# First feed-forward matrix in seven block products, its squares kept in DRAM, second matrix summed in eight PSUM banks

## The chip, the cores and the metric

The kernel runs on one core of a Trainium2 chip. The metric is the device time of one execution in microseconds (us). TensorE (PE in the profile) multiplies, VectorE (DVE), ScalarE (ACT) and GpSimd (POOL) work element by element, and SyncE (SP) issues nearly all transfers. PEld is TensorE's loading of the stationary operand, SPq the issuing of transfers on SP.

## The reference, cut to what matters

One layer of an encoder: three mixers, a gated merge, an output projection, then a feed-forward part and a final norm. Only the feed-forward part and its neighbours matter here:

```
x = x + merged @ w_out                       # (1024, 1024) @ (1024, 1024)
hf = rms_norm(x, ffn_norm_w)                 # 1024 tokens, 1024 features
x = x + square(relu(hf @ w_up)) @ w_down     # w_up (1024, 4096), w_down (4096, 1024)
return rms_norm(x, final_norm_w)
```

All of it is in float32.

## The kernel before

Every product of full precision is made of three passes. A float32 operand is split into a high part, which ScalarE casts (`L139`), and a low part, which VectorE or GpSimd gets by subtracting the high part from the original (`L140`). A matmul of operands a and b is then a-high b-high, a-high b-low and a-low b-high, summed in PSUM (`gemm_steps`, `gemm`). All matmuls go through `L81`, all transposes through `L84`, all transfers through `ld` on SP (`L97`).

The kernel is written as one list of operations. A planner simulates it and decides the order in which each engine runs its own; tiles are given out of pools with a fixed number of slots, and an operation that writes a tile waits until the slot's former tile has been read for the last time. Between `pe.pin = True` and `pe.pin = False` TensorE keeps the order of the program text.

**Output projection.** For each of eight blocks m of 128 tokens, 48 matmuls (two halves of 512 columns, eight k, three passes) give `x2`, to which the residual is added (`L1137`). `x2` is stored to `x2_d` in DRAM, squared and summed on ScalarE, and scaled in place by VectorE (`L1140`) into the normalised `hf`. `transposed(m, g)` then turns four 128 by 128 squares of it into one PSUM bank of the pool `ps_mm` (two banks) and splits them into `hfh` and `hfl`, in two pieces of 128 by 256: two casts on ScalarE, two subtractions on VectorE. I call one such call a turn. Eight turns (m = 0 to 3) are done inside the projection, the other eight between the first matmuls of the feed-forward part, one after every six matmuls.

**Feed-forward.** The 4096 hidden columns are cut into 32 tiles of 128, taken in 16 blocks of FB = 2. For each tile, `w_up`'s 1024 by 128 piece is loaded as `w_raw` (two slots) and split; `up` makes, for each half f of 512 tokens, 24 matmuls of 128 by 512 into one of six PSUM banks (`ps`), and then Relu on ScalarE (`L1159`), the square on VectorE (`L1160`) and the split into `ah`, `al`. The two matching 128 by 1024 rows of `w_down` are loaded as `w_raw` and split, the low part on GpSimd. `down` then makes, for each of eight token blocks and two column halves, six matmuls into a bank, and VectorE adds the bank to `o` in SBUF (`L1167`).

**End.** In the last block, after each `down`, ScalarE squares and sums `o` (`L1230`), GpSimd multiplies the first half by the final weight (`L1233`), `factor` makes the norm's factor, and `finish` scales the two halves (ScalarE, and VectorE in `L1183`) and stores them.

Pools: `U1` has 22 slots and `U2` 18 slots of 4 KB per partition; `wst` holds `w_raw`, `w_hi` and `w_lo`, two slots each; `sc` holds small working tiles (tags `g_l` and `g_t`, two slots each).

Of the kernel before, what the change touches and what calls it, by code (L numbers as in the profile page):

```python
# [24 lines left out]
FB = 2  # L25
# [45 lines left out]
class TensorE:  # L71


    def __init__(self, tc):
        self.tc, self.pin = tc, False
# [11 lines left out]
def hybrid_block(tc, x, mem, mix_norm_w, w_in, dn_conv_w, dn_a_log, dn_dt_bias, dn_norm_w, q_norm_w, k_norm_w,  # L87
# [107 lines left out]
    x2_d = [dram.tile([P, D], F32, name=f"x2_d{m}") for m in range(8)]  # L195

# [916 lines left out]
    hfh = [[None] * 4 for _ in range(2)]  # L1113
    hfl = [[None] * 4 for _ in range(2)]

    def transposed(m, g):
        t = slice((m % 4) * P, (m % 4 + 1) * P)
        ps = ps_mm()
        for j in range(4):
            pe.transpose(ps[:, j * P:(j + 1) * P], xs[m][:, (4 * g + j) * P:(4 * g + j + 1) * P], ident)  # L1120
        pv = ps.rearrange("p (k t) -> p k t", k=4)
        for q in range(2):
            split(hfh[m // 4][2 * g + q][:, :, t], hfl[m // 4][2 * g + q][:, :, t], pv[:, 2 * q:2 * q + 2])

    xs = []
    for m in range(8):
# [14 lines left out]
        if m % 4 == 3:  # L1141
            for k in range(4):
                hfh[f2][k] = ut("hfh", F32R, (P, 2, 512), True)
                hfl[f2][k] = ut("hfl", F32R, (P, 2, 512), True)
        if m >= 4:
            transposed(m - 4, 0)
            transposed(m - 4, 1)
# [3 lines left out]
    def up(w, f, ah, al_, between=()):  # L1151
        c = slice(f * 512, (f + 1) * 512)
        ps = ps2()
        pairs = [(w[0][:, k], w[1][:, k], hfh[f][k // 2][:, k % 2], hfl[f][k // 2][:, k % 2]) for k in range(8)]
        for i, _ in enumerate(gemm_steps(ps, pairs)):
            if i % 6 == 5 and between:
                transposed(*between.pop(0))
        r = sc.tile([P, 512], F32, name="f_r", tag="g_t")
        act.activation(out=r, in_=ps, func=AF.Relu)  # L1159
        dve.tensor_tensor(out=r, in0=r, in1=r, op=ALU.mult)  # L1160
        split(ah[:, c], al_[:, c], r)

    def down(m, c, a, wd):
        t = slice(m * P, (m + 1) * P)
        ps = ps2()[:, :c.stop - c.start]
        gemm(ps, [(a[k][0][:, t], a[k][1][:, t], wd[k][0][:, c], wd[k][1][:, c]) for k in range(FB)])
        dve.tensor_tensor(out=o[m][:, c], in0=o[m][:, c], in1=ps, op=ALU.add)  # L1167
# [22 lines left out]
    lwb = None  # L1190
    for blk in range(32 // FB):
        a, wu = [], []
        for ft in range(FB):
            wu.append(wunit(w_up[:, (blk * FB + ft) * P:(blk * FB + ft + 1) * P], 8, P))
            a.append((ut("ah", F32R), ut("al", F32R)))
            if blk > 0 or ft > 1:
                up(wu[ft], 0, *a[ft])
                up(wu[ft], 1, *a[ft])
            elif ft == 1:
                pe.pin = True  # L1200
                turns = [(m, g) for m in range(4, 8) for g in range(2)]
                up(wu[0], 0, *a[0], turns)
                up(wu[1], 0, *a[1], turns)
                pe.pin = False
                up(wu[0], 1, *a[0])
                up(wu[1], 1, *a[1])
        wd = []
        for k in range(FB):
            raw = wst.tile([P, 8, P], F32, name="w_raw", tag="w_raw").rearrange("p k c -> p (k c)")
            r = (blk * FB + k) * P  # L1210
            ld(out=raw, in_=w_down[r:r + P])
            two = blk % 2 == 1 and k == FB - 1
            wd.append((ut("wdh", F32R, two=two), ut("wdl", F32R, two=two)))
            split(*wd[k], raw, gp)
        if blk == 0:
            for m in range(8):
                o[m] = ut("o")
                ld(out=o[m], in_=x2_d[m])
        if blk == 32 // FB - 1:
            lwb = sc.tile([P, D], F32, name="lwb", tag="g_l")  # L1220
            ld(out=lwb, in_=final_norm_w.unsqueeze(0).broadcast_to([P, D]))
        for m in range(8):
            last = blk == 32 // FB - 1
            cs = (slice(0, 512), slice(512, 1024)) if not (last and m == 7) else (slice(0, 512), slice(512, 768), slice(768, 1024))
            if last:
                ss3[m] = sml.tile([P, 4], F32, name="ss3", tag="ss3", bufs=4)
            for j, c in enumerate(cs):
                down(m, c, a, wd)
                if last:
                    act.activation(out=sc.tile([P, 512], F32, name="jk3", tag="g_t")[:, :c.stop - c.start], in_=o[m][:, c],  # L1230
                                   func=AF.Square, accum_out=ss3[m][:, j:j + 1])
                    if j == 0:
                        gp.tensor_tensor(out=o[m][:, c], in0=o[m][:, c], in1=lwb[:, c], op=ALU.mult)  # L1233
            if last and m < 6:
                rs3[m] = factor(m, len(cs))
                finish(m)
    for m in (6, 7):
        rs3[m] = factor(m, len(cs) - 7 + m)
# [31 lines left out]
```

## Time and profile before

| | before |
|---|---|
| median of 3 runs | 1942.31 us (1937.68 to 1945.56) |
| profiled execution, its own time | 1945.84 us |
| its span, first to last instruction | 1944.0 us |
| mean granted TensorE clock | 0.989 |
| PE busy | 98% of the span, 10233 matmuls and transposes |
| DVE, ACT, POOL busy | 59%, 39%, 14% |
| DMA | 207.29 MB, mean 107 GB/s |

The span is the stretch that the profile covers; the profiled execution's time is 1.84 us longer. PE's busy time is the union of matmuls whose ends are modelled and which overlap, so the duration of one matmul is not what it costs; what it costs is the distance from one start to the next. The granted clock is given as a share of 2.4 GHz.

### The profile page before, as it was taken

How to read it: one execution, taken by the hardware profiler on the slowest of the kernel's cores; microseconds unless marked ns; L12 is line 12 of the kernel's file. 1: busy time of each engine (PE TensorE's matmuls, PEld its weight loads, DVE VectorE, ACT ScalarE, POOL GpSimd, SP SyncE). 2: the span in 40 equal slices, each digit the busy share in tenths (PEclk: the TensorE clock that was granted, in tenths of full speed). 3: DMA queues.
4: the chain of work that ended last, by engine and by line, in shares of the span. 5: the costliest groups of instructions: out<-in, count | busy, mean ns of one | idle time of the engine just before them, and what ended most of it. 6: DMA issues, size and time to landing. Idle time of an engine off the chain costs nothing.

```text
span 1944.0 us, 26261 instructions
## 1 busy us (share of the span) xinstructions
PE 1899.3 (98%) x10233; PEld 1609.5 (83%) x10233; DVE 1142.3 (59%) x1744; ACT 756.1 (39%) x1523; POOL 271.6 (14%) x230
## 2 busy tenths in 40 slices
PE   6999999999999999999999999999999999999997
PEld 5888778988988888888888878888888888888886
DVE  4677899993676666666635563444444434444446
ACT  4453434653546666666632131312121222112124
POOL 1003131231340000000001510101010101001013
PEclk8999999998999999999999999999999999999998
DMA  7235664566653222222255473311111202111113
GB/s 150 73 103 166 202 187 149 155 185 182 189 142 120 77 90 79 87 77 84 67 181 202 142 203 122 141 55 44 44 54 33 64 24 78 41 55 49 39 44 87
DMA packets 232750, 207.29 MB, mean 107 GB/s; under 512 B 44785, under 2 KB 196529, under 8 KB 232114
## 3 DMA queue, kind: packets, MB, share of 16 engines
q1 hardware_dynamic: 232306, 205.08, 35.1%
q8 instruction: 81, 1.33, 0.3%
q10 hardware_dynamic: 320, 0.52, 0.1%
q14 instruction: 43, 0.35, 0.1%
HBM read 148.39 MB, written 57.18 MB: 106 GB/s over the span
## 4 chain that ended last, share of the span: by engine, by line
PE 89%; DVE 4%; DMA 3%; issue 1%; ACT 1%; SPq 0%; POOL 0%; POOLq 0%; DVEq 0%; ACTq 0%
PE ps L81 40%; PE ps_mm L81 29%; PE ps_t L84 4%; PE ps_dn L81 4%; PE ps_sm L81 3%; PE ps_t L81 3%; PE ps_s L81 3%; PE ps_sp L81 2%; DMA xt<-in_x_dram 1%; DMA xs_d<-dd 1%; DMA w_raw<-in_w_out_dram 1%; DMA X<-xs_d 1%; DVE c_acc L409 1%; DVE o L1183 0%; SPq L97 0%
## 5 line engine op out<-in xcount | busy, mean ns | idle before, releaser
L81 PE MATMUL ps_mm<-hTh,w_hi 128*128 128x512 f32 x704 | 285.5, 406 | 5.2 <-ACT hTh L139 4.7
L81 PE MATMUL ps_mm<-hTl,w_hi 128*128 128x512 f32 x704 | 284.0, 403 | 0.0
L81 PE MATMUL ps_mm<-hTh,w_lo 128*128 128x512 f32 x704 | 277.5, 394 | 3.0 <-DVE w_lo L140 3.0
L1167 DVE TENSOR_TENSOR o<-o,ps 128x512 f32<-128x512 f32 (+1 forms) x257 | 170.9, 683 | 93.5 <-PE ps L81 92.7
L81 PE MATMUL ps<-hfh,w_hi 128*128 128x512 f32 x512 | 199.4, 391 | 0.0
L81 PE MATMUL ps<-wdh,al 128*128 128x512 f32 (+1 forms) x514 | 199.4, 388 | 0.0
L81 PE MATMUL ps<-wdl,ah 128*128 128x512 f32 (+1 forms) x514 | 199.4, 388 | 0.0
L81 PE MATMUL ps<-hfl,w_hi 128*128 128x512 f32 x512 | 199.3, 389 | 0.0
L81 PE MATMUL ps<-hfh,w_lo 128*128 128x512 f32 x512 | 199.3, 389 | 0.0
L81 PE MATMUL ps<-wdh,ah 128*128 128x512 f32 (+1 forms) x514 | 188.6, 388 | 0.0
L140 DVE TENSOR_TENSOR w_lo<-w_raw,w_hi 128x1024 fp32r<-128x1024 f32 x96 | 121.5, 1265 | 112.0 <-ACT w_hi L139 111.8
L1159 ACT ACTIVATE f_r<-ps 128x512 f32<-128x512 f32 x64 | 38.2, 597 | 358.9 <-PE ps L81 358.9
L139 ACT CAST w_hi<-w_raw 128x1024 fp32r<-128x1024 f32 x96 | 101.0, 1052 | 188.2 <-PE ps_mm L81 109.7
L1160 DVE TENSOR_TENSOR f_r<-f_r 128x512 f32<-128x512 f32 x64 | 55.4, 866 | 183.3 <-ACT f_r L1159 183.3
L140 POOL TENSOR_TENSOR wdl<-w_raw,wdh 128x1024 fp32r<-128x1024 f32 x32 | 76.3, 2395 | 601.4 <-ACT wdh L139 601.4
L81 PEld LDWEIGHTS ps_mm<-hTh,w_hi 128*128 128x128 f32 x704 | 133.5, 190 | 30.3 <-ACT hTh L139 5.1
L81 PEld LDWEIGHTS ps_mm<-hTh,w_lo 128*128 128x128 f32 x704 | 133.6, 190 | 28.7 <-DVE w_lo L140 3.2
L81 PEld LDWEIGHTS ps_mm<-hTl,w_hi 128*128 128x128 f32 x704 | 133.9, 190 | 20.8
L140 DVE TENSOR_TENSOR ptl<-ps_t,pth 128x512 fp32r<-128x512 f32 x128 | 86.6, 688 | 60.0 <-ACT pth L139 59.7
L81 PEld LDWEIGHTS ps<-wdh,ah 128*128 128x128 f32 x514 | 96.5, 188 | 20.5 <-DVE o L1167 0.6
L81 PEld LDWEIGHTS ps<-wdh,al 128*128 128x128 f32 x514 | 96.5, 188 | 19.8
L81 PEld LDWEIGHTS ps<-wdl,ah 128*128 128x128 f32 x514 | 96.4, 188 | 19.8
(288 smaller groups left out, 3838.3 us busy)
## 6 DMA issues: line engine op xcount, KB each, us to landing
w_raw<-in_w_in_dram SPq DMA_DIRECT2D x50, 512.0 KB
w_raw<-in_w_up_dram SPq DMA_DIRECT2D x32, 512.0 KB
w_raw<-in_w_down_dram SPq DMA_DIRECT2D x32, 512.0 KB
g_d<-gt SPq DMA_DIRECT2D x48, 256.0 KB
g_l<-g_d SPq DMA_DIRECT2D x24, 512.0 KB
w_raw<-in_w_branch_dram SPq DMA_DIRECT2D x12, 512.0 KB
y_raw<-y_d SPq DMA_DIRECT2D x12, 512.0 KB
xt<-in_x_dram SPq DMA_DIRECT2D x16, 256.0 KB
```

What stands on the lines that cost most here:

```text
L81: return self._put(self.tc.nc.tensor.matmul(*a, **k))
L84: return self._put(self.tc.nc.tensor.transpose(*a, **k))
L139: act.copy(out=hi, in_=src)
L140: (eng or dve).tensor_tensor(out=lo, in0=src, in1=hi.bitcast(F32), op=ALU.subtract)
L409: dve.scalar_tensor_tensor(out=acc[:, o], in0=xn[:, i], scalar=cw[:, ct, j:j + 1], in1=acc[:, o], op0=ALU.mult, op1=ALU.add)
L1159: act.activation(out=r, in_=ps, func=AF.Relu)
L1160: dve.tensor_tensor(out=r, in0=r, in1=r, op=ALU.mult)
L1167: dve.tensor_tensor(out=o[m][:, c], in0=o[m][:, c], in1=ps, op=ALU.add)
```

## The change

The first product, hidden = w_up transposed times hf transposed, is done by blocks. A unit u is a pair of tiles of hidden columns (256 columns, 16 units). Its weights are four blocks a11, a12 (first tile, feature halves) and a21, a22 (second tile), each 512 by 128; the tokens' side is four blocks b11, b21 (first 512 tokens, feature halves) and b12, b22 (second 512 tokens). Instead of eight block products there are seven, P1 to P7, of 12 matmuls of 128 by 512 each (four k, three passes). On the weights' side GpSimd makes four sums s1 to s4 per unit; on the tokens' side four sums T1 to T4 are made once, on GpSimd for the first two token blocks and on VectorE for the others. All seven weight blocks and seven token blocks are split into high and low parts: the token blocks stay in SBUF as `hs` (28 tiles, 16 in `U2` and 12 in `U1`), the weight blocks pass through the other slots of `U1`. Four token blocks now have two turns each as before (B11, B21), and 20 more turns (T3, T2, T1, B22, T4 for each of four blocks) stand between the 48 matmuls of P1 and P2 of the first two units, at a distance of four, three, two and two matmuls, in pinned order.

VectorE combines the products in `f_a` tiles: seven additions of a PSUM bank per unit, and four operations that do Relu and square at once. P1 is copied out by ScalarE. The two finished tiles of 128 by 1024 of a unit are stored to DRAM (`a_d`, 512 KB each). The first two units take P1 and P2 from a first load of one weight tile, and load both their tiles again for the rest.

The second product runs after the first is complete: for each half of 512 output columns, eight PSUM banks (six `ps2`, two `ps_mm`) hold the sums of the eight token blocks over all 32 k. Per k, the tile of `a_d` (512 KB) and the 128 by 512 piece of `w_down` (256 KB) are loaded and split, the latter's low part on GpSimd; k goes in groups of KG = 4, and within a group TensorE goes through the eight token blocks with 12 matmuls each. So `a_d` is read and split twice. `o` is added to once per block and half. In the last group of the second half, `factor` and `finish` follow each block; GpSimd's multiplication by the final weight is done in the first half only.

The diff, with the loops whose text is given above cut:

```diff
-    hfh = [[None] * 4 for _ in range(2)]
-    hfl = [[None] * 4 for _ in range(2)]
-    def transposed(m, g):
+    hs = {}
+    def turned(name, src, m):
+        if name not in hs:
+            hs[name] = [[ut("hs", F32R, (P, 2, 512), two=name in ("B11", "B21", "T3", "T2")) for i in range(2)] for _ in range(2)]
         ps = ps_mm()
         for j in range(4):
-            pe.transpose(ps[:, j * P:(j + 1) * P], xs[m][:, (4 * g + j) * P:(4 * g + j + 1) * P], ident)
+            pe.transpose(ps[:, j * P:(j + 1) * P], src[:, j * P:(j + 1) * P], ident)
...
+    turns = []
+    for m in range(4):
+        e = gp if m < 2 else dve
+        b11, b21, b12, b22 = xs[m][:, 0:512], xs[m][:, 512:1024], xs[m + 4][:, 0:512], xs[m + 4][:, 512:1024]
+        t3 = sc.tile([P, 512], F32, name="t3", tag="g_t")
+        e.tensor_tensor(out=t3, in0=b22, in1=b12, op=ALU.subtract)
+        e.tensor_tensor(out=b12, in0=b12, in1=b11, op=ALU.subtract)
+        e.tensor_tensor(out=b11, in0=t3, in1=b11, op=ALU.add)
+        e.tensor_tensor(out=b21, in0=b21, in1=b11, op=ALU.subtract)
+        turns += [("T3", t3, m), ("T2", b11, m), ("T1", b12, m), ("B22", b22, m), ("T4", b21, m)]
...
+    def halves(src, two=False):
+        w = ut("ws", F32R, (P, 2, 4, P), two=two)
+        split(w[:, 0], w[:, 1], src)
+        return w
...
+        gp.tensor_tensor(out=s1, in0=a21, in1=a22, op=ALU.add)
+        gp.tensor_tensor(out=s2, in0=s1, in1=a11, op=ALU.subtract)
+        gp.tensor_tensor(out=s3, in0=a11, in1=a21, op=ALU.subtract)
+        gp.tensor_tensor(out=s4, in0=a12, in1=s2, op=ALU.subtract)
+        for name, src in (("P6", s2), ("P2", a12), ("P7", s3), ("P4", a22), ("P5", s1), ("P3", s4)):
+            if name not in ws:
+                ws[name] = halves(src)
+    RHS = {"P1": "B11", "P2": "B21", "P3": "B22", "P4": "T4", "P5": "T1", "P6": "T2", "P7": "T3"}
+    def product(ws, name, between=(), every=4):
+        ps, w, (bh, bl) = ps2(), ws[name], hs[RHS[name]]
+        i = 0
+        for k in range(4):
+            for lw, rb in ((w[:, 0, k], bh), (w[:, 0, k], bl), (w[:, 1, k], bh)):
+                pe.matmul(ps, lhsT=lw, rhs=rb[k // 2][:, k % 2], start=i == 0, stop=i == 11)
+                i += 1
+                if i % every == 0 and between:
+                    turned(*between.pop(0))
+        return ps
+    def square(t):
+        dve.scalar_tensor_tensor(out=t, in0=t, scalar=0.0, in1=t, op0=ALU.max, op1=ALU.mult)
...
+        def rest(self):
+            r0, r1 = self.r0, ut("f_a", F32, (P, 2, 512), two=not self.lead)
+            add(r1[:, 1], r0[:, 1], product(self.ws, "P7"))
+            add(r1[:, 0], r1[:, 1], product(self.ws, "P4"))
+            square(r1[:, 0])
+            ps = product(self.ws, "P5")
+            add(r0[:, 1], r0[:, 1], ps)
+            add(r1[:, 1], r1[:, 1], ps)
+            square(r1[:, 1])
+            ld(out=a_d[2 * self.u + 1], in_=r1.rearrange("p f t -> p (f t)"))
+            add(r0[:, 1], r0[:, 1], product(self.ws, "P3"))
+            square(r0[:, 1])
+            ld(out=a_d[2 * self.u], in_=r0.rearrange("p f t -> p (f t)"))
+    pe.pin = True
+    lead = [Unit(0, True, "jk"), Unit(1, True)]
+    lead[0].p1(turns)
+    lead[1].p1(turns, 3)
+    lead[0].p2(turns, 2)
+    lead[1].p2(turns, 2)
...
+    for half in range(2):
+        c0 = half * 512
+        ps = [ps2() if m < 6 else ps_mm() for m in range(8)]
+        for kg in range(32 // KG):
+            a, wd = [], []
+            for k in range(kg * KG, (kg + 1) * KG):
+                raw = wst.tile([P, 8, P], F32, name="w_raw", tag="w_raw").rearrange("p k c -> p (k c)")
+                ld(out=raw, in_=a_d[k])
+                a.append((ut("ah", F32R, two=k % 2 == 0), ut("al", F32R, two=k % 2 == 0)))
+                split(*a[-1], raw)
+                raw = sc.tile([P, 512], F32, name="d_raw", tag="g_t")
+                ld(out=raw, in_=w_down[k * P:(k + 1) * P, c0:c0 + 512])
+                wd.append(ut("wd", F32R, (P, 2, 512), two=k % 2 == 1))
+                split(wd[-1][:, 0], wd[-1][:, 1], raw, gp)
...
-                down(m, c, a, wd)
+                        pe.matmul(ps[m][:, c], lhsT=ah[:, t], rhs=w[:, 0, c], start=kg == 0 and i == 0, stop=False)
+                        pe.matmul(ps[m][:, c], lhsT=ah[:, t], rhs=w[:, 1, c], start=False, stop=False)
+                        pe.matmul(ps[m][:, c], lhsT=al[:, t], rhs=w[:, 0, c], start=False, stop=last and i == KG - 1)
+                    dve.tensor_tensor(out=o[m][:, oc], in0=o[m][:, oc], in1=ps[m][:, c], op=ALU.add)
```

The eight loads of `o` from `x2_d` (512 KB each) move from the first feed-forward block to the start of the second product.

## Rows read from the trace of the kernel before

**Rows 1.** The page's busy times, and its chain of work that ended last
```profile
PE 1899.3 (98%) x10233; PEld 1609.5 (83%) x10233; DVE 1142.3 (59%) x1744; ACT 756.1 (39%) x1523; POOL 271.6 (14%) x230
...
PE 89%; DVE 4%; DMA 3%; issue 1%; ACT 1%; SPq 0%; POOL 0%; POOLq 0%; DVEq 0%; ACTq 0%
```
**Rows 2.** Stretches: busy us and count of PE, PEld, DVE, ACT, POOL; clock; DMA share, GB/s
```profile
1000.00:1100.00 100.00, 100.00 (x443) 82.79 (x442) 46.74 (x51) 18.79 (x19) 23.59 (x17) 1.00 0.52 173
1300.00:1400.00 100.00, 100.00 (x443) 82.81 (x442) 46.77 (x64) 19.43 (x27) 9.54 (x4) 1.00 0.18 53
...
1925.00:1944.00 19.00, 6.21 (x34) 5.19 (x32) 12.77 (x21) 8.86 (x23) 7.78 (x9) 0.74 0.63 166
```
**Rows 3.** TensorE in order of time, second product: a matmul and the twelfth after it
```profile
1400.05 0.39 PE L81 MATMUL ps<-wdh,al 128*128 128x512 f32 x1
...
1402.77 0.39 PE L81 MATMUL ps<-wdh,al 128*128 128x512 f32 x1
```
**Rows 4.** TensorE in order of time, two turns among first-product matmuls
```profile
1241.11 0.60 PE L84 MATMUL ps_mm<-ca,x 128*128 128x128 f32 x4
1241.46 0.48 PE L81 MATMUL ps<-hfh,w_hi 128*128 128x512 f32 x1
...
1242.93 0.60 PE L84 MATMUL ps_mm<-ca,x 128*128 128x128 f32 x4
1243.29 0.48 PE L81 MATMUL ps<-hfh,w_hi 128*128 128x512 f32 x1
```
**Rows 5.** ScalarE and VectorE in order of time, the split of one turn
```profile
1241.74 0.37 ACT L139 CAST hfh<-ps_mm 128x256 fp32r<-128x256 f32 x1 [0.33 <-PE ps_mm L84]
1242.61 0.38 ACT L139 CAST hfh<-ps_mm 128x256 fp32r<-128x256 f32 x1 [0.49 <-DVE hfl L140]
...
1243.02 0.42 DVE L140 TENSOR_TENSOR hfl<-ps_mm,hfh 128x256 fp32r<-128x256 f32 x1 [0.44 <-ACT hfh L139]
```
**Rows 6.** VectorE in order of time, three operations without a wait between
```profile
1132.14 0.69 DVE L140 TENSOR_TENSOR mgl<-g_acc,mgh 128x512 fp32r<-128x512 f32 x1
1132.74 0.69 DVE L1099 TENSOR_TENSOR g_acc<-g_acc,g_l 128x512 f32<-128x512 f32 x1
1133.34 0.68 DVE L1098 SCALAR_TENSOR_TENSOR g_l<-g_l,ps 128x512 f32<-128x512 f32 x1
```
**Rows 7.** GpSimd in order of time, one addition of 128 by 512 beside a busy VectorE
```profile
1108.67 1.62 POOL L1099 TENSOR_TENSOR g_acc<-g_acc,g_l 128x512 f32<-128x512 f32 x1 [1.81 <-DVE g_l L1098]
```
**Rows 8.** GpSimd and VectorE in order of time, about 1344
```profile
1341.03 4.75 POOL L140 TENSOR_TENSOR wdl<-w_raw,wdh 128x1024 fp32r<-128x1024 f32 x2 [41.17 <-ACT wdh L139]
...
1344.04 2.28 DVE L1160 TENSOR_TENSOR f_r<-f_r 128x512 f32<-128x512 f32 x1 [3.37 <-ACT f_r L1159]
```
**Rows 9.** A 512 KB load: its issue on SP, and the cast that waits for it
```profile
1118.69 0.33 SPq L97 DMA_DIRECT2D w_raw<-in_w_out_dram  x1
...
1123.11 1.05 ACT L139 CAST woh<-w_raw 128x1024 fp32r<-128x1024 f32 x1 [1.45 <-DMA w_raw<-in_w_out_dram]
```
**Rows 10.** Groups by shape between 1300 and 1900: busy us, mean ns
```profile
L140 DVE TENSOR_TENSOR w_lo<-w_raw,w_hi 128x1024 fp32r<-128x1024 f32 x27 | 33.1, 1225 | 57.4 <-ACT w_hi L139 57.4
...
L139 ACT CAST ah<-f_r 128x512 fp32r<-128x512 f32 x55 | 34.1, 621 | 62.0 <-DVE f_r L1160 62.0
```
**Rows 11.** VectorE in order of time: an addition, then what waits for its store
```profile
1228.85 0.69 DVE L1137 SCALAR_TENSOR_TENSOR x<-ps,x 128x512 f32<-128x512 f32 x1 [4.75 <-PE ps L81]
...
1232.92 1.29 DVE L1140 SCALAR_TENSOR_TENSOR x<-x,rs,fwb 128x1024 f32<-128x1024 f32 x1 [0.56 <-DMA x_d<-x]
```
**Rows 12.** The end in order of time: TensorE, ScalarE, VectorE
```profile
1930.93 0.28 PE L81 MATMUL ps<-wdh,al 128*128 128x256 f32 x1
...
1936.80 0.19 ACT L1230 ACTIVATION_READ_ACCUMULATOR jk<-o 128x1 f32 x1
...
1932.33 1.75 DVE L1183 SCALAR_TENSOR_TENSOR o<-o,rs,lwb 128x512 f32<-128x512 f32 x1
1934.01 0.68 DVE L1167 TENSOR_TENSOR o<-o,ps 128x512 f32<-128x512 f32 x1
...
1938.59 0.75 DVE L1183 SCALAR_TENSOR_TENSOR o<-o,rs,lwb 128x512 f32<-128x512 f32 x1 [0.73 <-POOL rs L136]
```

More of the change, by code (lines that the diff above doesn't have):

```diff
@@ L24 @@
 FILL = (3, 4, 5)
-FB = 2
+KG = 4
 LEAD = (12, 12)
@@ L195, in hybrid_block @@
     x2_d = [dram.tile([P, D], F32, name=f"x2_d{m}") for m in range(8)]
+    a_d = [dram.tile([P, S], F32, name=f"a_d{i}") for i in range(32)]
     ph1 = ExitStack()
@@ L1140, in hybrid_block @@
         dve.scalar_tensor_tensor(out=x2, in0=x2, scalar=rs, in1=fwb, op0=ALU.mult, op1=ALU.mult)
[L1141 to L1144, printed above, removed]
         if m >= 4:
-            transposed(m - 4, 0)
-            transposed(m - 4, 1)
-    o, ss3, rs3 = [None] * 8, {}, {}
[L1151 to L1167, printed above, removed]
+            turned("B11", xs[m - 4][:, 0:512], m - 4)
+            turned("B21", xs[m - 4][:, 512:1024], m - 4)
+    turns = []
[8 more added lines that the diff above has]
+        turns += [("T3", t3, m), ("T2", b11, m), ("T1", b12, m), ("B22", b22, m), ("T4", b21, m)]
@@ new lines, in add, with __init__, p1, p2 @@
+    def add(out, a, b):
+        dve.tensor_tensor(out=out, in0=a, in1=b, op=ALU.add)
+    def square(t):
+        dve.scalar_tensor_tensor(out=t, in0=t, scalar=0.0, in1=t, op0=ALU.max, op1=ALU.mult)
+    class Unit:
+        def __init__(self, u, lead=False, tag="g_l"):
+            self.u, self.ws, self.r0, self.lead = u, {}, None, lead
+            if lead:
+                raw = w_raw(2 * u)
+                self.ws = {"P1": halves(raw[:, 0:4], True), "P2": halves(raw[:, 4:8])}
+            else:
+                weights(u, self.ws)
+            self.t = sc.tile([P, 512], F32, name="f_t", tag=tag, **({"bufs": 1} if tag == "jk" else {}))
+        def p1(self, *a):
+            act.copy(out=self.t, in_=product(self.ws, "P1", *a))
+        def p2(self, *a):
+            ps = product(self.ws, "P2", *a)
+            self.r0 = self.r0 or ut("f_a", F32, (P, 2, 512), two=True)
+            add(self.r0[:, 0], self.t, ps)
+            square(self.r0[:, 0])
+        def p6(self):
+            ps = product(self.ws, "P6")
+            self.r0 = self.r0 or ut("f_a", F32, (P, 2, 512), two=True)
+            add(self.r0[:, 1], self.t, ps)
+        def rest(self):
[11 more added lines that the diff above has]
+            ld(out=a_d[2 * self.u], in_=r0.rearrange("p f t -> p (f t)"))
@@ L1169, in factor @@
+    pe.pin = True
[4 more added lines that the diff above has]
+    lead[1].p2(turns, 2)
+    for t in turns:
+        turned(*t)
+    pe.pin = False
+    for un in lead:
+        weights(un.u, un.ws)
+        un.p6()
+        un.rest()
+    for u in range(2, 16):
+        un = Unit(u)
+        un.p1()
+        un.p6()
+        un.p2()
+        un.rest()
     def factor(m, j):
@@ L1188, in finish @@
             ld_rows(o[m], out, m, store=True)
[L1190 to L1215, printed above, removed]
-            for m in range(8):
[L1217 to L1227, printed above, removed]
-                down(m, c, a, wd)
[L1229 to L1236, printed above, removed]
@@ L1237, in hybrid_block @@
     for m in (6, 7):
-        rs3[m] = factor(m, len(cs) - 7 + m)
+        rs3[m] = factor(m, 2)
     finish(7)
```

37 lines of the change are left out of this document (35 added, 2 removed).

## The prediction

> **What bounds the kernel now.** I read the busy times and the chain first, then stretches, then single instructions. The page puts 98% of the span and 89% of the chain on PE [rows 1]. In the feed-forward part, every stretch of 100 us that I asked for is full of PE work at a granted clock of 1.00, which is the 2.4 GHz level, with VectorE busy about 47 of 100 and the transfers at 18% [rows 2]. So TensorE sets the pace there, and a change is worth what it takes off or adds to TensorE, unless something else becomes late. The reader must not take a matmul's 0.39 us for its cost: starts lie 2.72 us apart over twelve matmuls, 0.2267 us each [rows 3], and 443 in 100 us say the same [rows 2]. Only at the very end is TensorE not the bound: its last matmul starts at 1930.93, and 13 us pass until the span's end, in which VectorE works off a backlog [rows 2, 12].
>
> **The first product.** Before: 32 tiles by two halves by 24 matmuls, 1536. After: 16 units by seven products by 12, 1344. That is 192 fewer, and 192 by 0.2267 is 43.5 us off. The second product keeps 1536 matmuls, all of 512 columns but for the last twelve, which were of 256; there only the order changes.
>
> The Trainium skill, page "TensorE: Matmul & The Clock Gate", section "Back-to-back issue gap", gives about 131 ns as the sustained distance for 512 columns. The trace shows 226.7 ns; by the page's figure the 192 matmuls would be worth 25 us and the forecast below 18 us higher, and I keep the measured one.
>
> **The turns.** There were 16, there are 28: the eight inside the projection stay, eight behind it become twenty. Two turns with six matmuls between start 1.82 us apart [rows 4]; six matmuls are 1.36, so a turn costs TensorE 0.46 us. Twelve more: plus 5.5 us.
>
> They also come closer together. On TensorE alone a turn would come every four, three or two matmuls: 1.37, 1.14 or 0.91 us. A turn's split alternates between ScalarE and VectorE: cast, subtraction, cast, subtraction, where the second cast waits for the first subtraction; from the transposes' start at 1241.11 to the last subtraction's end at 1243.44 it is 2.33 us [rows 4, 5]. With two banks that is one turn per 1.17 us if two turns overlap perfectly. For the sixteen turns of the three denser products the lag is then 4 by 0.03 plus 12 by 0.26, some 3 us. VectorE has other work in the same stretch: the last normalisation (1.3), four differences for the last token block (2.4), two additions and two squares (2.4), at 0.60 each [rows 6]; I let half of these 6 us fall into the chain: 6 us of stall in all. Its ends: none, if VectorE's other work falls between; and 15, if two turns don't overlap at all (20 by 1.73, the four conversions, against 20 us of TensorE work, that is 48 by 0.2267 plus 20 by 0.46).
>
> The token sums are otherwise covered: for the first two blocks GpSimd makes them while the projection still runs, where a block takes 48 by 0.2267, or 10.9 us, against four operations of up to 1.62 [rows 7]; the third block's fall in the same cover on VectorE.
>
> **The units.** A unit takes TensorE 84 by 0.2267, 19.0 us, and that must cover everything else. VectorE: seven low parts, seven additions, four squares, 18 at 0.60, 10.8 us [rows 6]. ScalarE: seven casts and a copy of 0.62 [rows 10], 5 us. GpSimd: four sums of up to 1.62, 6.5 us [rows 7]. Weights: `U1` keeps 10 slots beside the 12 token tiles, so a weight block can be written once the product ten before it is done and is wanted nine products, 24.5 us, later. Two loads one behind the other (4.4 us for a lone one [rows 9], some 7 for both), three sums (4.9) and a split (1.2) are 13 us. Results: `U2` keeps two slots. The earlier tile of a unit is stored after three VectorE operations behind P5 (1.8 us); a store of 512 KB lands at most 3.4 us after its data is ready [rows 11]; the next unit first writes its tile after P3, P1 and P6, 8.2 us. On SP the store waits for the square with the next loads of weights behind it, but those are wanted 24 us later. And should VectorE come late, six banks hold 16 us of products. So the units cost nothing beyond their matmuls. Without that cover, each us by which VectorE's unit passes 19.0 costs 16 us.
>
> **Between the products.** In the last unit, `o` takes eight slots of `U1` first; the second and fourth tile of `a_d` and the first and third of `w_down` get theirs only as P4 and P5 end. After P4, TensorE has P5 and P3 left, 5.4 us, then 2 us of matmuls per block on the first three k. In that time the second tile is split (2.3), the fourth loaded (4.4) and split (2.3): 9.0 against 7.4, and 4 MB of `o` run beside it. I take 5 us of stall; the ends are none (if tiles come free earlier) and 14 (four k served at 3.5 us each, the second product's service time below, with nothing ahead).
>
> **The second product.** A k takes TensorE 24 by 0.2267, 5.4 us, in each half. It needs 768 KB, 145 GB/s; between 1000 and 1100 the queues moved 173 GB/s at a share of 0.52 without holding up TensorE [rows 2]. A slot of `w_raw` is held for a load (4.4 [rows 9]), a cast and a subtraction (1.05 and 1.23 [rows 9, 10]) and an issue (0.33), 7.0 us; with two slots 3.5 us per k, under 5.4. ScalarE has 1.7 us per k, VectorE 1.2, GpSimd 1.6. Cost: nothing. VectorE loses 257 additions into `o` and gets 16; they lay beside TensorE, so that is worth nothing, except at the end.
>
> **The end.** Before, each block of the last group cost VectorE two additions, and a scaling that took 1.75 beside GpSimd's multiplication, 0.75 without it [rows 12]. After, in the second half, it is one addition, two tiny operations and 0.75, some 1.7 us, under TensorE's 2.72 per block. So the end follows the last matmul: its own 0.39, the addition 0.69, the square and sum 0.8, semaphores 0.1, and then from the end of the last sum at 1936.99 to 1944.0 as before, 7.0: 9.0 us instead of 13.1. Minus 4 us; ends minus 5 and nothing.
>
> **Sum.** −43.5 + 5.5 + 6 + 5 − 4 = −31.0. The profiled execution took 1945.84 and would take 1914.8; the median of the runs shown lies 3.5 below that execution, so I forecast 1911. With all ends favourable it is −43.0, 1899; with all unfavourable −9.5, 1933.
>
> **Rivals.** (1) VectorE becomes the bound of the units. For it: a VectorE operation with two SBUF inputs that started beside GpSimd's two took 2.28 us instead of 0.69 and ended with them [rows 8], so it waited for GpSimd. If all of GpSimd's 6.5 us per unit were lost to VectorE, 10.8 becomes 17.3, still under 19.0; waiting for weight sums in its queue would have to add the rest. At 21 us per unit it costs 31 us: 1942, no change.
> The Trainium skill, page "SBUF — State Buffer", section "Who interferes with whom", has this as a rule: the pair of ports is an exclusive lock, and the later instruction blocks fully. The trace agrees; by the rule alone the unit stays TensorE's.
> (2) The second product becomes bound by its loads, the other side. What it has against it is the count above; for it, that `a_d` is read back twice, loads and 4 KB rows share one queue with `w_down`'s, and the two slots leave no more than one load in flight while the other is split. It decides at a load of 8.2 us, 1.9 times the measured one; the forecast's gain is gone at 9.2. At 10 us a k takes 6.3 instead of 5.4, 64 times: plus 55, 1966.
> (3) The two seams are worse than my ends, because TensorE, starved for several us, also gets the clock that the last stretch shows after its last matmul (0.74 on average [rows 2]): 1938, no change.
> (4) A matmul costs its 0.39 us, and 192 are worth 75 us: 1880. The starts speak against it.
>
> **Chances.** Forecast 0.78 (own range 1899 to 1933); (1) 0.06; (2) 0.09; (3) 0.05; (4) 0.02. A difference under 0.5%, 9.7 us, can't be told from none. Faster 0.80, same 0.11, slower 0.09. From 1898 to 1936 leaves out (1), (2), (4) and half of (3), under 2 in 10.
>
> **What would show it.** In the profile after: 1344 first-product matmuls 0.227 apart, PE without idle time from the second unit to the last; in the stretch after the projection, idle TensorE before transposes, some 6 us; a gap of some 5 us where the second product begins; VectorE at 60 to 90% in the units and under 40% in the second product, where DMA stands near 150 GB/s; and some 9 us from the last matmul's start to the end. Casts of `a_d` tiles waiting for transfers with TensorE waiting behind them would show (2); TensorE waiting for VectorE's additions or low parts inside units, (1). The prediction is wrong if the planner's order puts a late operation ahead of an urgent one on a strictly ordered engine, which I can't see from the trace of before.

## The result, and the profile after

The changed kernel takes 1920.88 us (median of 4 runs, 1916.88 to 1923.65), beside 1943.47 us before on the same chip: a ratio of 0.9887, 95% interval 0.9857 to 0.9917. It is faster, by 22.6 us where 31 were forecast. The profiled executions say the same: spans of 1921.9 and 1944.0 us, 22.1 apart.

The page's busy times and chain after, to be held against [rows 1]:

```profile
PE 1869.7 (97%) x10083; PEld 1582.3 (82%) x10083; DVE 1154.8 (60%) x1727; ACT 801.6 (42%) x1609; POOL 405.0 (21%) x334
...
PE 88%; DVE 5%; DMA 3%; ACT 1%; issue 1%; POOL 0%; SPq 0%; POOLq 0%; DVEq 0%; ACTq 0%
```

Three stretches after, with the columns of [rows 2]: the turns behind the projection, the units up to the last one, the second product:

```profile
1229.20:1276.00 46.80, 34.56 (x152) 25.62 (x152) 32.49 (x62) 19.44 (x52) 13.20 (x9) 0.82 0.23 68
1276.00:1564.00 288.00, 287.88 (x1270) 238.39 (x1271) 205.07 (x278) 73.52 (x123) 84.11 (x58) 1.00 0.39 127
1564.00:1913.00 349.00, 348.96 (x1540) 288.40 (x1538) 99.20 (x100) 114.19 (x160) 114.85 (x77) 1.00 0.46 149
```

The second and third are full of TensorE work at the full clock. The first is not: TensorE is without work for 12.2 of 46.8 us, and its granted clock is 0.82 on average. Nearly all that the change gave back is there. TensorE in that stretch, in order of time (start, us, operation, and in brackets the idle time before it and what ended it):

```profile
1229.22 1.42 PE L81 MATMUL ps<-hs,ws 128*128 128x512 f32 x4
...
1232.87 0.60 PE L84 MATMUL ps_mm<-ca,x 128*128 128x128 f32 x4
1233.23 1.17 PE L81 MATMUL ps<-hs,ws 128*128 128x512 f32 x4
1238.14 1.08 PE L84 MATMUL ps_mm<-ca,x 128*128 128x128 f32 x4 [3.74 <-issue]
1238.87 1.63 PE L81 MATMUL ps<-hs,ws 128*128 128x512 f32 x3
...
1249.81 0.63 PE L84 MATMUL ps_mm<-ca,x 128*128 128x128 f32 x4 [1.94 <-issue]
```

Each gap stands before the four transposes of a turn: they wait for a bank whose last turn has not been split. (For the gap of 3.74 us the profile names no releaser; the low part that frees the bank ended at 1238.03, 0.11 us before the transposes.) After the gap of 3.74 us the same four transposes take 1.08 instead of 0.60 us and three matmuls 1.63 us, where three took 0.94 at the full clock (a row of a later run below): TensorE had gone to its 1.2 GHz level. VectorE and GpSimd at the longest gap, each in order of time:

```profile
1230.32 0.15 DVE L135 TENSOR_SCALAR rsq_t<-ss 128x1 f32<-128x1 f32 x1 [0.69 <-ACT jk L222]
...
1232.15 1.13 DVE L1153 TENSOR_TENSOR t<-x 128x512 f32<-128x512 f32 x1 [0.28 <-PE ps_mm L84]
1233.20 0.41 DVE L140 TENSOR_TENSOR hs<-ps_mm,hs 128x256 fp32r<-128x256 f32 x1
1233.54 1.44 DVE L1154 TENSOR_TENSOR x<-x,x 128x512 f32<-128x512 f32 x1
1235.42 2.28 DVE L1142 SCALAR_TENSOR_TENSOR x<-x,rs,fwb 128x1024 f32<-128x1024 f32 x1 [0.44 <-POOL rs L136]
1237.62 0.41 DVE L140 TENSOR_TENSOR hs<-ps_mm,hs 128x256 fp32r<-128x256 f32 x1
1237.96 1.42 DVE L1155 TENSOR_TENSOR x<-t,x 128x512 f32<-128x512 f32 x1
...
1245.61 0.69 DVE L1153 TENSOR_TENSOR t<-x 128x512 f32<-128x512 f32 x1 [0.41 <-PE ps_mm L84]
...
1231.44 1.29 POOL L1179 TENSOR_TENSOR w_s<-w_raw 128x512 f32<-128x512 f32 x1 [12.12 <-DMA w_raw<-in_w_up_dram]
1232.69 1.75 POOL L1181 TENSOR_TENSOR w_s<-w_raw 128x512 f32<-128x512 f32 x1
1234.39 0.99 POOL L136 TENSOR_TENSOR rs<-rsq_t,mhalf 128x1 f32<-128x1 f32 x1
1235.36 1.26 POOL L1180 TENSOR_TENSOR w_s<-w_s,w_raw 128x512 f32<-128x512 f32 x1
```

The low part that would free the bank is the one at 1237.62. Ahead of it on VectorE stand a difference of the third token block (`L1154`), stretched to 1.44 us, and the last normalisation (`L1142`), which waits for its factor and then takes 2.28 us. The factor (`L136` on GpSimd) had its input at 1230.47 and ran only at 1234.39, behind two weight sums, the first of which waited for its load until 1231.44. GpSimd runs its operations in the order that the planner gave it. The third block's first difference (`L1153`) ran only at 1232.15, released by transposes (`L84`): the tile t3 that it writes has two slots, and both held T3 of the first two blocks until the first was turned. The fourth block's waited in the same way until 1245.61.

The end after, in order of time, against [rows 12]:

```profile
1913.00 0.39 PE L81 MATMUL ps_mm<-wd,al 128*128 128x512 f32 x1
...
1913.99 0.68 DVE L1320 TENSOR_TENSOR o<-o,ps_mm 128x512 f32<-128x512 f32 x1
...
1915.23 0.19 ACT L1321 ACTIVATION_READ_ACCUMULATOR jk<-o 128x1 f32 x1
...
1916.53 0.75 DVE L1281 SCALAR_TENSOR_TENSOR o<-o,rs,lwb 128x512 f32<-128x512 f32 x1 [0.73 <-POOL rs L136]
```

From the last matmul's start to the span's end it is 8.9 us, where it was 13.1. VectorE keeps up: the scaling takes 0.75 us and follows its factor.

### The profile page after: what moved, and what is told of

The parts are those of the page before. It is cut to its first block, busy times and chain, and to the rows that moved or that the text cites. A ratio compares the mean times of both kernels' runs of the same rounds, so it can differ in the third digit from the quotient of the medians.

```text
span 1921.9 us, 26681 instructions
## 1 busy us (share of the span) xinstructions
PE 1869.7 (97%) x10083; PEld 1582.3 (82%) x10083; DVE 1154.8 (60%) x1727; ACT 801.6 (42%) x1609; POOL 405.0 (21%) x334
## 3 DMA queue, kind: packets, MB, share of 16 engines
q1 hardware_dynamic: 252818, 256.47, 43.5%
## 4 chain that ended last, share of the span: by engine, by line
PE 88%; DVE 5%; DMA 3%; ACT 1%; issue 1%; POOL 0%; SPq 0%; POOLq 0%; DVEq 0%; ACTq 0%
PE ps L81 34%; PE ps_mm L81 34%; PE ps_t L84 4%; PE ps_dn L81 4%; PE ps_sm L81 3%; PE ps_t L81 3%; PE ps_s L81 3%; PE ps_sp L81 2%; DMA xt<-in_x_dram 1%; DMA w_raw<-in_w_out_dram 1%; PE ps_mm L84 1%; DVE c_acc L410 1%; DMA xs_d<-dd 1%; DVE w_lo L140 0%; SPq L97 0%
## 5 line engine op out<-in xcount | busy, mean ns | idle before, releaser
L81 PE MATMUL ps<-hs,ws 128*128 128x512 f32 x1344 | 314.5, 394 | 0.3 <-ACT hs L139 0.2
L81 PEld LDWEIGHTS ps<-hs,ws 128*128 128x128 f32 x1344 | 253.0, 190 | 52.0 <-ACT hs L139 0.8
L81 PE MATMUL ps<-wd,ah 128*128 128x512 f32 x768 | 236.4, 389 | 0.0
L140 DVE TENSOR_TENSOR al<-w_raw,ah 128x1024 fp32r<-128x1024 f32 x64 | 83.7, 1309 | 208.5 <-ACT ah L139 116.0
L81 PEld LDWEIGHTS ps<-wd,ah 128*128 128x128 f32 x768 | 144.0, 188 | 30.5 <-POOL wd L140 0.8
L140 POOL TENSOR_TENSOR wd<-d_raw,wd 128x512 fp32r<-128x512 f32 x64 | 102.5, 1604 | 228.6 <-ACT wd L139 228.6
L81 PE MATMUL ps<-wd,al 128*128 128x512 f32 x384 | 148.9, 389 | 0.0
L139 ACT CAST pth<-ps_t 128x512 fp32r<-128x512 f32 x128 | 74.1, 584 | 49.1 <-PE ps_t L84 48.9
L900 ACT ACTIVATE pm<-ps_s,nmx 128x1024 f32<-128x1024 f32 x64 | 71.6, 1119 | 41.1 <-DVE nmx L899 41.1
L899 DVE TENSOR_REDUCE nmx<-ps_s 128x1 f32<-128x1024 f32 x64 | 78.2, 1221 | 17.5 <-PE ps_s L81 16.5
```

Of the source, the lines that this page charges most:

```text
L81: return self._put(self.tc.nc.tensor.matmul(*a, **k))
L139: act.copy(out=hi, in_=src)
L140: (eng or dve).tensor_tensor(out=lo, in0=src, in1=hi.bitcast(F32), op=ALU.subtract)
L899: dve.tensor_reduce(out=nmx, in_=ps, axis=AX.X, op=ALU.max, negate=True)
L900: act.activation(out=p_out, in_=ps, func=AF.Exp, bias=nmx, accum_out=sm)
```

## The experiments

The measure that they share is the loss: the time from the first matmul of the first product to the first of the second, less 1344 by 0.2267 and 20 by 0.46, that is less 313.9 us. In the changed kernel it is 1564.57 − 1229.22 − 313.9 = 21.5 us. Where the stretch begins differs by up to 9 us between the profiled executions (1220.6 to 1230.0); I compare stretches and not spans for that reason, and have not looked into what shifts it. "Waits" is TensorE's idle time with a releaser in the stretch, read from its timeline, and "longest" the longest of them. "Factor" is how long after the stretch's first matmul GpSimd began the last normalisation's factor. Times are medians, each ratio is to the kernel before on the same chip. Each loss is read from one profiled execution. Executions of one kernel lie up to 10 us apart (no differences: 1907.25 to 1917.25, the profiled one the slowest), and no run shows how much of that falls into the stretch, so small differences between losses prove nothing.

| run | us | ratio, interval | stretch from, to | loss | waits | longest | factor |
|---|---|---|---|---|---|---|---|
| changed kernel | 1920.88 | 0.9887, 0.9857 to 0.9917 | 1229.22, 1564.57 | 21.5 | 12.3 | 3.74 | 5.2 |
| t3 slots | 1913.30 | 0.9849, 0.9826 to 0.9872 | 1229.07, 1556.57 | 13.6 | 8.8 | 1.92 | 1.3 |
| no sums for the first units | 1913.28 | 0.9851, 0.9832 to 0.9870 | 1222.58, 1551.34 | 14.9 | 8.9 | 1.93 | 1.3 |
| four banks | 1910.64 | 0.9837, 0.9818 to 0.9857 | 1229.59, 1553.10 | 9.6 | 5.8 | 3.34 | 5.5 |
| no differences | 1911.58 | 0.9834, 0.9808 to 0.9860 | 1229.94, 1558.70 | 14.9 | 9.5 | 3.20 | 5.0 |
| no sums, no differences | 1906.26 | 0.9822, 0.9807 to 0.9838 | 1220.59, 1544.13 | 9.6 | 6.4 | 1.00 | 1.4 |
| slots and banks | 1904.28 | 0.9814, 0.9800 to 0.9829 | 1224.75, 1544.11 | 5.5 | 4.3 | 1.72 | 1.3 |
| and differences on GpSimd | 1907.04 | 0.9826, 0.9810 to 0.9843 | 1229.96, 1553.09 | 9.2 | 6.6 | 2.74 | 5.9 |
| slots, banks, spread | 1907.54 | 0.9825, 0.9800 to 0.9850 | 1227.78, 1547.82 | 6.1 | 4.9 | 1.73 | 1.3 |
| spread alone | 1913.68 | 0.9857, 0.9837 to 0.9877 | 1221.81, 1552.49 | 16.8 | 11.6 | 3.69 | 5.1 |

One thing differs between these runs that no edit was made for. In five of them, the changed kernel among them, the planner put the factor behind one or two weight sums, so that it came 5.0 to 5.9 us into the stretch, and there the longest wait is 2.74 to 3.74 us. In the other five it came after 1.3 or 1.4 us, and the longest wait is 1.00 to 1.93 us. No run moves the factor alone, so what its place is worth by itself is not shown; where an edit changed it, I say so.

**Slots for t3.**

```diff
-        t3 = sc.tile([P, 512], F32, name="t3", tag="g_t")
+        if m < 2:
+            t3 = sc.tile([P, 512], F32, name="t3", tag="g_t")
+        else:
+            t3 = wst.tile([P, 2, 4, P], F32, name="t3", tag=("w_hi", "w_lo")[m - 2])[:, 0].rearrange("p k c -> p (k c)")
```

> The changed kernel with one thing moved: the difference tile t3 of the third and fourth token block gets slots of its own (in the weight pool), so that its operations need not wait until the first two blocks' T3 have been turned. In the changed kernel the stretch from the first first-product matmul to the first second-product matmul is 336 us, of which 1344 matmuls at 0.2267 and 20 turns at 0.46 explain 314; 22 us are lost, all of them ahead of 1276 us. Theory A (the differences come late, in front of the low parts on VectorE, because t3 has two slots): the third block's four operations go back into the projection, the gaps of 3.7 and 1.9 us before transposes shrink, and 8 us or more of the 22 come back: about 1912 us. Theory B (GpSimd's weight sums lock VectorE out): 0 to 3 us. Theory C (two banks with an alternating split set the turns' rate whatever VectorE does): 0 to 3 us.

The loss fell by 7.9 us, nearly the 8 that theory A gave. That the differences come late because of t3's slots is shown: the third block's first one ran at 1221.16, inside the projection, and not 2.9 us into the stretch. That all of the 7.9 us comes from this is not shown, for with the slots the planner also put the factor ahead of the weight sums:

```profile
1230.40 0.55 POOL L136 TENSOR_TENSOR rs<-rsq_t,mhalf 128x1 f32<-128x1 f32 x1 [11.23 <-DVE rsq_t L135]
```

And 13.6 us stay.

**No weight sums for the first two units.**

```diff
+        if u < 2:
+            for name, src in (("P6", a21), ("P7", a11), ("P4", a22), ("P5", a21), ("P3", a22)):
+                ws[name] = halves(src)
+            return ws
         gp.tensor_tensor(out=s1, in0=a21, in1=a22, op=ALU.add)
```

> The changed kernel without GpSimd's eight weight sums of the first two units: their weight blocks are split straight from the loaded pieces, so P3, P5, P6 and P7 of these units multiply other numbers; everything else stays. Theory B: VectorE's operations beside these sums took 1.1 to 2.3 us instead of 0.7 to 1.3, about 6 us in all, and the normalisation's factor waited on GpSimd behind them; 6 to 10 of the 22 us come back, about 1912 us. Theory A: 2 us or less, 1919. Theory C: nothing, 1921.

The loss fell by 6.6 us, within what theory B gave. In the changed kernel's rows the operations that ran beside these sums are longer by 4.7 us in all, not by the 6 that I wrote down. The edit takes away two things together: that stretching, and the sums' place ahead of the factor, which here began at 1223.90. So the sums cost time in this stretch, but how much comes from either of the two is not separated.

**Four banks for the turns.**

```diff
-        ps = ps_mm()
+        nt[0] += 1
+        ps = ps2() if name not in ("B11", "B21") and nt[0] % 2 else ps_mm()
```

> The changed kernel, with every second of the twenty turns put into a bank of the six-bank pool instead of the two-bank one, so that four or more turns can be under way. Theory C (banks and the alternating split limit the turns): the lost 22 us fall under 10, about 1908 us. Theories A and B (VectorE has too much to do ahead of the low parts): the turns are still late by as much, 18 to 22 us lost, 1917 to 1921.

The loss fell to 9.6 us, as theory C gave, which the other two had ruled out. With more banks, though, the work itself comes to the front. The stretch behind the projection in this run, the transposes behind a gap of 3.34 us, and VectorE up to the low part that ended it:

```profile
1230.00:1260.00 30.00, 24.15 (x130) 19.72 (x130) 27.47 (x56) 17.08 (x49) 12.98 (x9) 0.89 0.24 76
...
1240.47 0.80 PE L84 MATMUL ps_mm<-ca,t 128*128 128x128 f32 x4 [3.34 <-DVE hs L140]
...
1235.69 2.30 DVE L1143 SCALAR_TENSOR_TENSOR x<-x,rs,fwb 128x1024 f32<-128x1024 f32 x1 [1.03 <-POOL rs L136]
1237.91 1.75 DVE L1156 TENSOR_TENSOR x<-t,x 128x512 f32<-128x512 f32 x1
1239.58 0.41 DVE L140 TENSOR_TENSOR hs<-ps,hs 128x256 fp32r<-128x256 f32 x1
1239.91 0.41 DVE L140 TENSOR_TENSOR hs<-ps_mm,hs 128x256 fp32r<-128x256 f32 x1
```

VectorE is busy 27.5 of 30 us. Banks let TensorE run ahead of the split, they don't make the split less.

**No differences.**

```diff
-        e.tensor_tensor(out=t3, in0=b22, in1=b12, op=ALU.subtract)
-        e.tensor_tensor(out=b12, in0=b12, in1=b11, op=ALU.subtract)
-        e.tensor_tensor(out=b11, in0=t3, in1=b11, op=ALU.add)
-        e.tensor_tensor(out=b21, in0=b21, in1=b11, op=ALU.subtract)
-        turns += [("T3", t3, m), ("T2", b11, m), ("T1", b12, m), ("B22", b22, m), ("T4", b21, m)]
+        turns += [("T3", b22, m), ("T2", b11, m), ("T1", b12, m), ("B22", b22, m), ("T4", b21, m)]
```

> The changed kernel without the sixteen operations that make the token sums: T1 to T4 are turned from the unsummed blocks, so six of the seven products multiply other numbers; the turns themselves, the weight sums and everything else stay. Theory A: with no differences on VectorE, the turns are held by the split alone, and 12 us or more of the 22 come back, 1909 or less. Theory B: 3 to 6 us. Theory C: 5 us at most, 1916 or more.

6.6 us came back, between the theories' numbers. (Four products, P4 to P7, multiply other numbers here, not six.) By its loss this run gains less than the one with slots (7.9 us), although the work is gone altogether; by their times the two cannot be told apart (1911.58 and 1913.30 us, with overlapping intervals). They differ in the factor too, which stood behind two weight sums here and not there. So the comparison doesn't show that lateness was all that the differences cost; it shows that most of the loss has other causes.

**Neither sums nor differences.** Both edits above together.

> Neither the first two units' weight sums nor the sixteen token sums are made: weight and token blocks are used unsummed, so most products multiply other numbers. Two banks, the turns, their splits and the normalisation stay. If two banks with an alternating split hold the turns back by themselves (theory C), 10 us or more of the 22 stay lost: 1909 or more. If the chain costs what the prediction gave it (some 3 us, with the last normalisation 5), it is 6 us or less: 1905 or less.

9.6 us stay lost, nearly theory C's 10, and well over what the prediction gave the chain. The time is less clear: 1906.26 us lies under the 1909 that went with theory C and next to the 1905 of the other side. The two edits nearly add up: 6.6 and 6.6 of 21.5 would leave 8.3. What remains has no difference and no sum in it, and the clock of the stretch is 1.00: turns in two banks, with a split that alternates between two engines. Three turns in a row on TensorE, and VectorE beside them, in this run:

```profile
1230.37 0.62 PE L84 MATMUL ps_mm<-ca,x 128*128 128x128 f32 x4
1230.75 0.94 PE L81 MATMUL ps<-hs,ws 128*128 128x512 f32 x3
1231.72 0.63 PE L84 MATMUL ps_mm<-ca,x 128*128 128x128 f32 x4
1232.10 0.70 PE L81 MATMUL ps<-hs,ws 128*128 128x512 f32 x2
1233.81 0.63 PE L84 MATMUL ps_mm<-ca,x 128*128 128x128 f32 x4 [1.00 <-DVE hs L140]
...
1231.14 0.76 DVE L140 TENSOR_TENSOR hs<-ps_mm,hs 128x256 fp32r<-128x256 f32 x2 [0.44 <-ACT hs L139]
1231.95 1.29 DVE L140 TENSOR_TENSOR ws<-w_raw,ws 128x512 fp32r<-128x512 f32 x2
1233.23 0.76 DVE L140 TENSOR_TENSOR hs<-ps_mm,hs 128x256 fp32r<-128x256 f32 x2
```

Two weight splits (`ws`, 1.29 us) stand between the low parts of two turns, and TensorE waits a microsecond. They are two of five such splits for the first unit in the stretch, which were in no term of the prediction's stretch.

**Slots and banks together.** The first and third edit.

> Slots of its own for the third and fourth t3 together with four banks for the turns. With four banks VectorE was busy 27.5 of the 30 us after the projection. If its amount of work is now the limit (theory D), moving the third block's differences out (2.4 us, and 1.5 us that they lost to GpSimd) takes the loss from 9.6 us to about 6: 1907. If late order and few banks are separate causes (8 and 12 us taken back alone), nearly nothing is left: 2 us or less, 1902.

5.5 us lost: near theory D's 6, and not the 2 of separate causes. Against the run with four banks the factor comes 4.2 us earlier here, so the differences' new place need not be the whole gain. This version beats both kernels: 1904.28 us, a ratio of 0.9814 (0.9800 to 0.9829), whose interval lies under the changed kernel's. The stretch of its turns has the full clock; its longest wait was 1.72 us:

```profile
1224.70:1256.00 31.30, 27.04 (x154) 21.21 (x154) 26.75 (x60) 20.25 (x55) 13.08 (x9) 1.00 0.36 110
```

**Differences on GpSimd as well.**

```diff
-        e = gp if m < 2 else dve
+        e = gp
```

> As the run with slots and banks together, and the third and fourth block's differences on GpSimd too. Theory D (VectorE's amount of work): 2.4 us less on VectorE in the stretch, loss about 4 us, 1905. Theory B (GpSimd's lock): GpSimd works 5 us longer beside VectorE's normalisation and weight splits, which gives as much back: 6 us or more lost, 1907 or more.

Theory B's side: the loss rose from 5.5 to 9.2 us. VectorE had less to do and was held up more, in two ways. The first is the order on GpSimd: the longest wait of TensorE stands behind VectorE's normalisation, which waited 3.39 us for a factor that GpSimd had put behind a weight sum, and that sum waited for its load. TensorE, VectorE and GpSimd there:

```profile
1240.42 1.09 PE L84 MATMUL ps_mm<-ca,t 128*128 128x128 f32 x4 [2.74 <-DVE hs L140]
...
1236.44 2.30 DVE L1143 SCALAR_TENSOR_TENSOR x<-x,rs,fwb 128x1024 f32<-128x1024 f32 x1 [3.39 <-POOL rs L136]
...
1234.61 1.29 POOL L1183 TENSOR_TENSOR w_s<-w_raw 128x512 f32<-128x512 f32 x1 [6.29 <-DMA w_raw<-in_w_up_dram]
1235.85 0.56 POOL L136 TENSOR_TENSOR rs<-rsq_t,mhalf 128x1 f32<-128x1 f32 x1
```

The second is what theory B is about: two weight splits that take 1.29 us took 3.43, while GpSimd made differences, and a low part of a turn beside a weight sum, from the same run:

```profile
1240.19 0.41 DVE L140 TENSOR_TENSOR hs<-ps,hs 128x256 fp32r<-128x256 f32 x1
...
1243.96 3.43 DVE L140 TENSOR_TENSOR ws<-w_s,ws 128x512 fp32r<-128x512 f32 x2 [0.97 <-ACT ws L139]
...
1240.05 1.27 POOL L1185 TENSOR_TENSOR w_s<-w_raw 128x512 f32<-128x512 f32 x1
...
1243.88 1.29 POOL L1159 TENSOR_TENSOR x<-t,x 128x512 f32<-128x512 f32 x1
1245.24 1.60 POOL L1160 TENSOR_TENSOR x<-x 128x512 f32<-128x512 f32 x1
```

The Trainium skill, page "SBUF — State Buffer", section "Who interferes with whom", says that a VectorE instruction with two SBUF inputs and a GpSimd instruction that reads SBUF exclude one another. The trace agrees: the low parts of turns, with one input in PSUM, kept their 0.41 us. How the rise of 3.7 us divides between the two ways is not shown.

**Turns spread**, on slots and banks, and alone. Fifteen turns ahead of the first unit's P6, the other five inside its P6 and P7:

```diff
...
+    late = [turns[i] for i in (15, 14, 19, 17, 18)]
+    turns = turns[:14] + [turns[16]]
...
-    lead[0].p2(turns, 2)
-    lead[1].p2(turns, 2)
-    for t in turns:
-        turned(*t)
-    pe.pin = False
+    lead[0].p2(turns, 3)
+    lead[1].p2(turns, 3)
     for un in lead:
         weights(un.u, un.ws)
-        un.p6()
-        un.rest()
+        un.p6(late)
+        un.rest(late)
+        pe.pin = False
```

> Slots, banks, and the turns spread: fifteen of the twenty stand at three or four matmuls' distance before P6 of the first unit, the other five between the matmuls of its P6 and P7, each ahead of the product that needs it. Theory D (VectorE's amount of work in a stretch that TensorE finishes sooner): TensorE's stretch grows by 24 matmuls, 5.4 us, while VectorE's work does not, so the 5.5 us still lost fall to 2.5 or less: 1901. If the loss only moves to P6 and P7, because seven weight splits of the first unit fall there as well, it stays near 5: 1904.

> The changed kernel with the turns spread in the same way, but with two banks and t3's two slots as they were. If the turns' distance is what matters, 10 us or more of the 21.5 come back, 1911 or less. If late differences and GpSimd's sums hold the turns back whatever their distance, it is 4 to 8 us: 1913 to 1917.

On slots and banks it brought nothing (6.1 for 5.5 us lost), near the 5 of its rival expectation, so theory D was wrong that more TensorE work in the stretch would cover VectorE's: the differences and the weight splits still come first. Alone it took 4.7 us off the loss, what the second expectation gave to late differences and sums that hold the turns back whatever their distance.

**Eight products.** The first product as before, its squares through DRAM and the second product as in the changed kernel:

```diff
...
+        r = fa[:, c]
         act.activation(out=r, in_=ps, func=AF.Relu)
         dve.tensor_tensor(out=r, in0=r, in1=r, op=ALU.mult)
-        split(ah[:, c], al_[:, c], r)
...
+        ld(out=a_d[ft], in_=a[ft])
```

> One part of the change undone: the first product as in the kernel before (1536 matmuls, eight turns behind the projection, Relu on ScalarE, square on VectorE), but with its squares stored to DRAM and the second product as in the changed kernel. If the working's terms are right one by one, this is the kernel before less the shorter end, 4 to 5 us: 1937, with the second product's matmuls 0.2267 us apart and nothing lost where it begins. Rival (reading the squares back twice costs something that the changed kernel hides in its sum): 1944 or more. Then the seven products must have brought more than 43.5.

1937.19 us, ratio 0.9980 (0.9971 to 0.9990): 4.1 us faster than before, the end alone: from the last matmul's start to the span's end it is 9.0 us in this run, where it was 13.1. From its first matmul (1224.79) to the first of the second product (1577.57) it is 352.8 us, where 1536 by 0.2267 and eight turns are 351.9; so neither the way through DRAM nor the start of the second product costs anything, though the loads run at 295 GB/s there:

```profile
1580.00:1600.00 20.00, 20.00 (x89) 16.54 (x89) 4.13 (x4) 7.08 (x9) 5.90 (x4) 1.00 0.82 295
```

The seven products with their turns are the rest: 16.3 us by the medians, some 18 by the ratios (0.9980 and 0.9887).

## Why the prediction was right, point by point, and where it was off

The measured time lies in the range, and the sign and mechanism were the forecast's: fewer matmuls at their distance of starts, less what the turns lose. A part of it is luck: one term came out 14.5 us dearer and another 4.6 us cheaper than forecast, which partly cancel; without the second it would have been some 1925 us, still in the range. Against the terms of its sum, from the profiled executions:

| term | forecast | measured |
|---|---|---|
| 192 matmuls fewer | −43.5 | −43.5 (1344 counted; 288 us of units full of work) |
| twelve more turns | +5.5 | +5.5 (same distances when nothing waits) |
| stall among the turns | +6 (0 to 15) | +20.5 |
| between the products | +5 (0 to 14) | +0.4 |
| units, second product | 0 | 0 |
| the end | −4 | −4.2 |
| sum | −31.0 | −21.3; the spans differ by 22.1 |

The stall is 21.5 less the 1.0 that the kernel before lost among its own turns (from 1229.71 to its first matmul of the second product at 1256.11, less 96 matmuls and eight turns). For the matmuls the table takes the distance of [rows 3]; what shows it to hold is that the last 1272 matmuls of the first product took 288.45 us (1276.12 to 1564.57), 0.2268 each.

**The mis-sized term is the stall among the turns**, 6 us with an end of 15, which measured 20.5. These steps of its working failed. "The third block's fall in the same cover on VectorE" was wrong: t3's two slots held them back, and the run that gave slots lost 7.9 us less, with whatever the factor's earlier place gave in it. "I let half of these 6 us fall into the chain" left out those four differences, five weight splits (3 us at 0.60), and that two-input operations stretch beside GpSimd's sums; leaving the sums out brought 6.6 us, again with the factor's place in it. The chain's own "some 3 us" was 9.6 with normalisation, weight splits, additions and squares beside it. The planner's order did what the prediction's last sentence feared and could not see: on GpSimd, weight sums stood ahead of the normalisation's factor, with the longest wait of the stretch behind it. And the clock: of the 21.5 us lost 12.3 are waits, and 9.2 are slower work, at a granted clock of 0.82; in the three runs whose stretch stayed at 1.00 the part beyond waits was 1.2 to 3.2 us. So by estimate some 6 to 8 us came from the clock, which the prediction had only in rival (3). The end of 15 was passed for that reason too. These shares overlap and don't sum; what is shown is what each edit brings, with what the planner changed along with it.

**Between the products** TensorE lost 0.4 us and not 5, though the transfers were as late as feared. The first cast of an `a_d` tile after the seam, and TensorE there:

```profile
1564.57 1.07 PE L81 MATMUL ps<-wd,ah 128*128 128x512 f32 x4
...
1566.05 1.05 ACT L139 CAST ah<-w_raw 128x1024 fp32r<-128x1024 f32 x1 [5.89 <-DMA w_raw<-a_d]
```

The load issued at 1558.46 was waited for until 1566.05, 7.6 us, behind the loads of `o`. But TensorE did not go block by block in the text's order there, which is two matmuls with `ah` and one with `al` over and over: it began with four with `ah`, and the regular pattern starts only at about 1573. So it worked on what had arrived, as far as the rows show (they don't name banks or k), and waited for nothing. I had taken the text's order for TensorE's.

**The units** cost nothing: VectorE was busy 205 of 288 us, 71%, where 10.8 to 17.3 of 19.0 was the count. GpSimd's hold shows without reaching TensorE: the Relu-and-square, with two SBUF inputs, took 960 ns on average, the additions out of PSUM 679 (rows grouped by shape, between 1300 and 1540):

```profile
L1205 DVE SCALAR_TENSOR_TENSOR f_a<-f_a 128x512 f32<-128x512 f32 x50 | 48.0, 960 | 0.0
L1202 DVE TENSOR_TENSOR f_a<-f_a,ps 128x512 f32<-128x512 f32 x62 | 41.2, 679 | 20.2 <-PE ps L81 20.2
```

That decides rival (1): VectorE did not become the bound of the units. (In [rows 8] the VectorE operation ended 0.54 us after GpSimd's two, not with them, which is what waiting for them would give.)

**The second product** cost nothing either, which rules out rival (2): 149 GB/s (145 counted), a share of 0.46, and a load of `a_d` (issue on SP, and the cast that waited for it) takes about 3.2 us, against the 8.2 from which it would have decided:

```profile
1700.84 0.32 SPq L97 DMA_DIRECT2D w_raw<-a_d  x1
...
1704.01 1.05 ACT L139 CAST ah<-w_raw 128x1024 fp32r<-128x1024 f32 x1 [1.28 <-DMA w_raw<-a_d]
```

**Rival (3)** was half right: one seam, not both, went past its end, and the clock fell; the gain was not eaten. **Rival (4)** is out: 192 by 0.39 would have shown 1880. **The end** came out as counted, in the changed kernel and, alone, in the run with eight products.

What stays open: what the factor's place on GpSimd is worth by itself, which one run of the changed kernel with only the factor ahead of the weight sums would show; and of the 5.5 us that slots and banks leave, I know that VectorE is busy 26.8 of 31.3 us there, not which of its operations would have to go.

## What to carry to other kernels

Price a saved matmul by the distance of starts in its own stretch; here that term and the long stretches came out to the microsecond, and the error lay in the two seams, most of it in one of 47 us. In a seam, list everything that each engine must do in it, also what belongs to the next stage, and ask of every operation that you call covered whether its output tile has a free slot at that time. Look also at the order on the engine that seems idle: a tiny operation behind one that waits for a load can hold up the rest. And after each experiment compare the order on every engine with the order before: an edit of one thing can make a planner move another. A wait on TensorE of some microseconds costs more than itself when the clock falls behind it; and work moved to GpSimd is not free for VectorE when both read two operands from SBUF.

## What the runs showed of the hardware that was not expected

Among waits of 3.74 us and less TensorE ran at half speed for a while (four transposes in 1.05 to 1.09 us instead of 0.60), and the stretch of 46.8 us averaged a granted clock of 0.82 although TensorE was busy in 34.6 of it. The runs with longest waits of 1.00, 1.72 and 1.73 us kept 1.00 in a stretch of that length, those with 1.92 and 1.93 us had 0.96 and 0.93; no run varies a wait alone, so no limit follows from this. Two VectorE subtractions that take 1.29 us took 3.43 beside GpSimd. And transfers of 260 GB/s (the changed kernel, 1540 to 1560, a share of 0.78) and of 295 GB/s (eight products, 0.82) did not hold up a TensorE that was 100% busy.
